# Every other pair of rows of the down blocks as seven products, and fewer low halves by adding DMA

## The chip, the cores and the metric

One NeuronCore of a Trainium2 chip runs the whole kernel. The metric is the time of one execution in device microseconds. Three runs of the kernel before took 2382.86, 2375.7 and 2385.11 us; the median, 2382.86, is the time before.

## What is computed

Two decoder layers on 256 tokens of width 2048 in float32. Each layer adds a mixer of attention heads and then an MLP to the residual x; a final RMSNorm ends it. The change touches the MLP alone:

```python
def squared_relu_mlp(h, w1, w2):
    return jnp.square(jax.nn.relu(h @ w1)) @ w2
...
    h = rmsnorm(x, ln_mlp[layer])
    x = x + squared_relu_mlp(h, mlp_w1[layer], mlp_w2[layer])
```

Here w1 is 2048 x 8192 and w2 is 8192 x 2048, 64 MB each in each layer.

## The kernel before

Every float32 operand is held as two fp32r halves: the high half is a cast, the low half is the operand less the high half. A product of two operands is three matmuls, high x high, high x low and low x high (`mm`, lines 180 to 186). `split` (149) makes both halves: ScalarE casts (150), VectorE subtracts (151). So most casts and subtracts, and most matmuls of the down products, carry these helper lines.

The MLP (`mlp`, 710) cuts the 8192 hidden columns into 16 units of 512, and the units into six chunks of 2, 3, 3, 3, 3 and 2 (`CHUNKS`, 713). A unit takes 8 up steps (`Up`, 780), one for each 256 rows of w1; each loads 512 KB, and its products go to four PSUM banks of the pool `acc` (811, 812). At the last of them `Unit.leave` (746) empties the banks: ScalarE copies and VectorE adds four times (750, 751), then ScalarE takes ReLU and square (752, 753). `Unit.build` (756) later makes the halves that the down products use as stationary operand, in parts that are done one a step.

The down product of a chunk goes by four blocks of 512 output columns, and in a block by pairs: a pair is 256 rows of w2, two to a unit, and one step. Two kinds of step exist. `Plain` (818) multiplies 2 row tiles x 2 token tiles x 512 columns: 12 matmuls of 512 columns. `Seven` (850) takes the same pair as a 2 x 2 by 2 x 2 product with seven products in place of eight: 21 matmuls of 256 columns, for which sums of weights (`sums`, 863, three VectorE adds into a tile T), sums of activations (the `s` tiles of `build`, 762 to 770) and a recombination at the block's end (`end`, 884: one ScalarE copy, six VectorE operations, two later adds into x) are needed. In the kernel before, the first three blocks of a chunk are all `Seven`, in four banks of the pools `psc` and `ptr`, and the fourth is all `Plain`, in the two banks of `psc`, from which VectorE adds into x (902). The last chunk is all `Plain` and stays as it is.

Raw weights come through six raw tiles of 512 KB (`raw_tile`, 143), loaded on SyncE's queue. High and low halves of 1024 columns take three tiles each (`half_tiles`, 146; tags wh and wl); steps of seven products take two wide tiles each (`wide_tiles`, 723; sh and sl). For the up steps of chunks 1 to 5 (`moved`), the low half is not made by VectorE: `early` (787) casts on ScalarE (791), writes the negated high half on ScalarE (792), and a DMA on GpSimd's queue adds the raw weights to it (793). The raw tile is free again when that DMA has landed.

The order of the work is written out by hand. `woven` (948) puts the up steps of chunk c + 1 between the down steps of chunk c, about one to one; that is a layer's woven stretch, 112 up and 112 down steps. The loop at 1001 then does, for the step at position p: load the step at p + 7, split the step at p + 2, the early halves of the step at p + 4, the sums of the step at p + 3, the products of p and what ends there, and one part of the waiting builds and adds (`later`). Each engine takes its instructions in that order.

Of the kernel before, what the change touches and what calls it, by code (L numbers as in the profile page):

```python
# [66 lines left out]
def decoder_trunk(ctx, tc, const, x_in, ln_mix, ln_mlp, ln_final, e_w_in, e_g_q, e_g_kv, e_w_uq, e_w_ukv, e_w_out,  # L67
# [10 lines left out]
    def nm(s):  # L78
        uid[0] += 1
        return f"{s}_{uid[0]}"  # L80
# [68 lines left out]
    def split(hi, lo, raw):  # L149
        nc.scalar.copy(hi, raw)  # L150
        nc.vector.tensor_tensor(lo, raw, hi.bitcast(F32), op=ALU.subtract)  # L151
# [558 lines left out]
    def mlp(layer, ss, done, tail=None):  # L710
# [3 lines left out]
        with ExitStack() as st:  # L714
# [21 lines left out]
            class Unit:  # L736
# [19 lines left out]
                def build(self):  # L756

                    def first():
                        self.halves = [pool.tile([P, 2, 8, 128], F32R, name=nm(h), tag=f"{h}{self.n}", bufs=1) for h in ("ah", "al")]
                        split(*(h[:, :, :4] for h in self.halves), self.a)  # L760

                    def second():
                        a = self.a
                        t = self.t = pool.tile([P, 2, 4, 128], F32, name=nm("s"), tag="s", bufs=1)
                        nc.vector.tensor_tensor(t[:, :, 0:2], a[:, :, 0:1].to_broadcast([P, 2, 2, 128]), a[:, :, 1:3], op=ALU.subtract)

                    def third():
                        a, t = self.a, self.t
                        nc.vector.tensor_tensor(t[:, :, 2], a[:, :, 1], t[:, :, 1], op=ALU.subtract)
                        nc.vector.tensor_tensor(t[:, :, 3], a[:, :, 3], t[:, :, 2], op=ALU.subtract)  # L770

                    def last():
                        split(*(h[:, :, 4:] for h in self.halves), self.t)

                    return [first] if self.c == len(CHUNKS) - 1 else [first, second, third, last]

                def slot(self, p, s):
                    return [h[:, p, s, :] for h in self.halves]

            class Up(Step):  # L780
# [6 lines left out]
                def early(self):  # L787

                    if self.moved:
                        hi, lo = self.w = half_tiles()  # L790
                        nc.scalar.copy(hi, self.raw)  # L791
                        nc.scalar.activation(lo, hi.bitcast(F32), AF.Copy, scale=-1.0)  # L792
                        nc.gpsimd.dma_start(lo, self.raw, accum_op=ALU.add)  # L793
# [56 lines left out]
            class Seven(Step):  # L850
# [5 lines left out]
                PRODUCTS = ((0, 0, 1, 1), (0, 1, 6, 6), (1, 0, 4, 5), (1, 1, 5, 4), (2, 0, 2, 7), (2, 1, 7, 2), (3, 0, 3, 3))  # L856

                def __init__(self, block, i, units, cs, c):
                    self.block, self.i, self.units, self.cs = block, i, units, cs
                    self.pairs = 2 * len(units)  # L860
                    self.src = rows(w2[:, cs], 4 * sum(CHUNKS[:c]) + 2 * i)

                def sums(self):
                    self.t = pool.tile([P, 1024], F32, name=nm("T"), tag="T", bufs=2)
# [10 lines left out]
                def product(self):  # L875
# [3 lines left out]
                    wh, wl = (w.rearrange("p (s n) -> p s n", n=256) for w in self.w)  # L879
                    for q, j, sa, sb in self.PRODUCTS:  # L880
                        mm(b["o"][q][:, j, :], self.units[i // 2].slot(i % 2, sa), (wh[:, sb - 1], wl[:, sb - 1]), i == 0 and j == 0,
                           i == self.pairs - 1, skip_group_check=True)

                def end(self):
# [3 lines left out]
                    (p1, p6), (p7, p5), (p4, p3), (p2, _) = ((b[:, 0, :], b[:, 1, :]) for b in o)  # L888
                    v = pool.tile([P, 2, 512], F32, name=nm("v"), tag="v", bufs=1)
                    c1, u2, u3, u4 = v[:, 0, 256:], v[:, 1, 256:], v[:, 0, :256], v[:, 1, :256]  # L890
                    nc.scalar.copy(c1, p1)
                    nc.vector.tensor_tensor(u2, p6, c1, op=ALU.subtract)
                    nc.vector.tensor_add(v[:, :, :256], o[1], u2.unsqueeze(1).to_broadcast([P, 2, 256]))
                    nc.vector.tensor_add(u2, p2, c1)
                    nc.vector.tensor_tensor(c1, p4, u3, op=ALU.subtract)
                    nc.vector.tensor_add(u3, p5, u3)
                    nc.vector.tensor_add(u4, p3, u4)
# [36 lines left out]
            def ups(c, moved):  # L934
                return [Up(u, i, moved) for u in units[c] for i in range(KT // 2)]

            def downs(c):
# [3 lines left out]
                for n in range(4):  # L941
                    block = {"of": psc}
                    cs = slice(n * 512, n * 512 + 512)
                    for i in range(2 * CHUNKS[c]):
                        seq.append(Seven(block, i, units[c], cs, c) if n < 3 else Plain(block, i, units[c], cs, c, True))
                return seq

            def woven(a, b):

                out, i = [], 0  # L950
                for j, s in enumerate(b):
                    while i < len(a) and i * len(b) <= j * len(a):
                        out.append(a[i])
                        i += 1
                    out.append(s)
                return out + a[i:]
# [143 lines left out]
```

## Time and profile before

| what | value |
|---|---|
| median of three runs | 2382.86 us |
| profiled execution: time, span of its instructions | 2385.53 us, 2383.8 us |
| mean granted TensorE clock, share of full speed | 0.977 |
| TensorE matmul busy | 2247.1 us |
| VectorE, ScalarE busy | 1574.4 us, 1443.8 us |
| read from HBM | 403.08 MB |
| mean rate of all DMA queues | 220 GB/s |

Busy time of an engine is the time in which one of its instructions runs; issuing and waiting do not count. Matmuls overlap, so a step is better measured from its first matmul to the first matmul of the next step. The granted clock is that of TensorE, as a share of 2.4 GHz. In the views, PE is TensorE, DVE is VectorE, ACT is ScalarE, POOL is GpSimd and SP is SyncE, a q after the name is its queue, and an arrow in a wait points to what ended it.

### The profile page before, as it was taken

Reading aid. Unit: us, or ns where it says so; the run is one execution under the profiler, and the core shown is the slowest. Engines: PE = TensorE matmul, PEld = TensorE weight load, DVE = VectorE, ACT = ScalarE, POOL = GpSimd, SP = SyncE. Lnnn points to the kernel's source line nnn. Section 1 sums busy time; section 2 is a strip of 40 time slices with the busy share of each in tenths; the row PEclk is TensorE's granted clock in tenths of the full one; section 3 lists DMA queues with packets and bytes.
Section 4 is the critical chain, followed back from the end, with each engine's and each line's share of the span. In section 5 each row is a group of like instructions: output and inputs, shape, how many; then the busy total and the mean of one; then the engine's idle time right before and its main releaser. Section 6 shows DMA issues by size and latency. Waiting matters only on the chain.

```text
span 2383.8 us, 35175 instructions
## 1 busy us (share of the span) xinstructions
PE 2247.1 (94%) x13590; PEld 1993.2 (84%) x13590; DVE 1574.4 (66%) x2505; ACT 1443.8 (61%) x1845; POOL 193.1 (8%) x228
## 2 busy tenths in 40 slices
PE   8999999898999999999999999998899999999898
PEld 7899988687888878788799999886788888887886
DVE  6777665555867767586675666555558577675866
ACT  6445444666867767676544444445677677776664
POOL 0000000011111111111000000001111111111110
PEclk9999999999999999999999999999999999999999
DMA  7554445699999999989565565456999999999884
GB/s 243 169 169 149 151 167 175 163 261 262 276 265 258 259 254 280 260 233 249 174 192 169 162 183 165 173 181 171 265 262 281 266 248 267 259 262 264 234 234 150
DMA packets 245860, 524.92 MB, mean 220 GB/s; under 512 B 18423, under 2 KB 23485, under 8 KB 245693
## 3 DMA queue, kind: packets, MB, share of 16 engines
q1 hardware_dynamic: 213436, 405.23, 51.3%
q0 software_dynamic: 32256, 117.45, 26.4%
q8 instruction: 106, 1.74, 0.3%
q14 instruction: 62, 0.50, 0.1%
HBM read 403.08 MB, written 2.10 MB: 170 GB/s over the span
## 4 chain that ended last, share of the span: by engine, by line
PE 52%; DMA 21%; DVE 12%; ACT 8%; issue 6%; SPq 0%; POOL 0%; DVEq 0%; ACTq 0%; POOLq 0%
PE bank L185 13%; PE bank L184 13%; PE bank L186 13%; DMA wl<-raw 11%; DMA raw<-in_mlp_w_dram 9%; PE bank L811 6%; DVE sl L151 4%; PE bank L812 3%; ACT wh L791 2%; ACT sh L150 2%; ACT wl L792 2%; DVE a L751 1%; DVE x L902 1%; ACT a L752 1%; DVE T L866 1%
## 5 line engine op out<-in xcount | busy, mean ns | idle before, releaser
L811 PE MATMUL bank<-xx,wh 128*128 128x512 f32 x2048 | 748.5, 403 | 5.0 <-DVE a L751 5.0
L812 PE MATMUL bank<-xx,wl 128*128 128x256 f32 x2048 | 587.2, 287 | 52.4 <-DMA wl<-raw 52.3
L151 DVE TENSOR_TENSOR wl<-raw,wh 128x1024 fp32r<-128x1024 f32 (+2 forms) x302 | 363.1, 1204 | 261.1 <-ACT wh L150 255.4
L150 ACT CAST wh<-raw 128x1024 fp32r<-128x1024 f32 (+2 forms) x302 | 311.2, 1033 | 351.9 <-PE bank L186 155.6
L184 PE MATMUL bank<-sh,ah 128*128 128x256 f32 (+1 forms) x1472 | 460.1, 313 | 35.4 <-DVE x L902 19.3
L185 PE MATMUL bank<-sl,ah 128*128 128x256 f32 (+1 forms) x1472 | 460.3, 313 | 15.5 <-DVE sl L151 15.3
L811 PEld LDWEIGHTS bank<-xx,wh 128*128 128x128 f32 x2048 | 393.6, 192 | 92.2 <-DVE a L751 7.2
L186 PE MATMUL bank<-sh,al 128*128 128x256 f32 (+1 forms) x1472 | 458.0, 311 | 8.1 <-DVE al L151 8.1
L812 PEld LDWEIGHTS bank<-xx,wl 128*128 128x128 f32 x2048 | 394.9, 193 | 69.6 <-DMA wl<-raw 67.0
L151 DVE TENSOR_TENSOR sl<-raw,sh 128x768 fp32r<-128x768 f32 (+1 forms) x241 | 248.7, 1032 | 241.6 <-ACT sh L150 240.8
L793 POOL DMA_DIRECT2D wl<-raw x224 | 192.9, 861 | 2120.3 <-ACT wl L792 1886.3
L791 ACT CAST wh<-raw 128x1024 fp32r<-128x1024 f32 x224 | 234.5, 1047 | 206.0 <-DMA raw<-in_mlp_w_dram 178.1
L184 PEld LDWEIGHTS bank<-sh,ah 128*128 128x128 f32 x1472 | 291.0, 198 | 60.6 <-ACT sh L150 13.6
L185 PEld LDWEIGHTS bank<-sl,ah 128*128 128x128 f32 x1472 | 291.3, 198 | 31.4 <-DVE sl L151 21.4
L186 PEld LDWEIGHTS bank<-sh,al 128*128 128x128 f32 x1472 | 291.9, 198 | 21.2 <-DVE al L151 9.1
L792 ACT ACTIVATE wl<-wh 128x1024 fp32r<-128x1024 f32 x224 | 237.6, 1061 | 7.1
L150 ACT CAST sh<-raw 128x768 fp32r<-128x768 f32 (+1 forms) x241 | 212.7, 883 | 44.6 <-PE bank L186 44.5
L150 ACT CAST sh<-T 128x1024 fp32r<-128x1024 f32 x168 | 176.2, 1049 | 67.3 <-DVE T L868 65.4
L185 PE MATMUL bank<-xx,wh 128*128 128x256 f32 x768 | 216.5, 282 | 0.0
L184 PE MATMUL bank<-xx,wh 128*128 128x256 f32 x768 | 216.3, 282 | 0.0
L186 PE MATMUL bank<-xx,wl 128*128 128x256 f32 x768 | 215.6, 282 | 0.0
L151 DVE TENSOR_TENSOR sl<-T,sh 128x1024 fp32r<-128x1024 f32 x168 | 205.6, 1224 | 11.7 <-ACT sh L150 7.2
(188 smaller groups left out, 3054.6 us busy)
## 6 DMA issues: line engine op xcount, KB each, us to landing
raw<-in_mlp_w_dram SPq DMA_DIRECT2D x510, 512.0 KB, 6.2
wl<-raw POOLq DMA_DIRECT2D x224, 512.0 KB, 7.1
raw<-in_o_w_in_dram SPq DMA_DIRECT2D x96, 512.0 KB, 3.8
raw<-in_e_w_in_dram SPq DMA_DIRECT2D x71, 512.0 KB, 3.5
raw<-in_e_w_out_dram SPq DMA_DIRECT2D x32, 512.0 KB, 3.5
raw<-in_o_w_out_dram SPq DMA_DIRECT2D x32, 512.0 KB, 3.5
raw<-in_e_w_uq_dram SPq DMA_DIRECT2D x8, 384.0 KB, 3.1
raw<-in_e_w_in_dram SPq DMA_DIRECT2D x8, 320.0 KB, 5.3
```

Source lines behind the costliest of these rows:

```text
L150: nc.scalar.copy(hi, raw)
L151: nc.vector.tensor_tensor(lo, raw, hi.bitcast(F32), op=ALU.subtract)
L184: nc.tensor.matmul(o, ah, bh, start=first, stop=False, **kw)
L185: nc.tensor.matmul(o, ah, bl, start=False, stop=False, **kw)
L186: nc.tensor.matmul(o, al, bh, start=False, stop=last, **kw)
L751: nc.vector.tensor_add(av[:, f], o[f][:, 0, :], av[:, f])
L752: nc.scalar.activation(self.a, self.a, AF.Relu)
L791: nc.scalar.copy(hi, self.raw)
L792: nc.scalar.activation(lo, hi.bitcast(F32), AF.Copy, scale=-1.0)
L793: nc.gpsimd.dma_start(lo, self.raw, accum_op=ALU.add)
L811: nc.tensor.matmul(u.o[f], wh[:, kk, fs], xx[:, k], start=k == 0, stop=False, skip_group_check=True)
L812: nc.tensor.matmul(u.o[f][:, 0, :], wl[:, kk, fs], xx[:, k, 0], start=False, stop=k == KT - 1, skip_group_check=True)
```

## The change

In all four blocks of chunks 0 to 4, even pairs are `Seven` and odd pairs are a new `Eight`: plain products that add to the last two of the same four banks, so that the seven products are laid out over the banks in another order and `end` recombines for all four blocks. Only the first pair of a unit needs sums of activations, so `build` has one part less and smaller ones. Of the eight up steps of a unit, numbers 1, 4 and 7 keep the adding DMA, with two tiles of their own for each half (mh, ml); the other five are split by ScalarE and VectorE two steps ahead. There is one T tile in place of two. `woven` now goes block by block: two up steps, then the block's pairs with the other up steps between them. A layer has 56 `Seven` and 56 `Eight` steps in its woven stretch, where it had 84 `Seven` and 28 `Plain`.

```diff
     def half_tiles(n=1024):
         return [wpool.tile([P, 1024], F32R, name=nm(h), tag=h, bufs=3)[:, :n] for h in ("wh", "wl")]
-    def split(hi, lo, raw):
+    def split(hi, lo, raw, on=nc.vector):
         nc.scalar.copy(hi, raw)
-        nc.vector.tensor_tensor(lo, raw, hi.bitcast(F32), op=ALU.subtract)
+        on.tensor_tensor(lo, raw, hi.bitcast(F32), op=ALU.subtract)
     class Weights:
...
                 def build(self):
                     def first():
-                        self.halves = [pool.tile([P, 2, 8, 128], F32R, name=nm(h), tag=f"{h}{self.n}", bufs=1) for h in ("ah", "al")]
-                        split(*(h[:, :, :4] for h in self.halves), self.a)
+                        self.halves = [pool.tile([P, 12, 128], F32R, name=nm(h), tag=f"{h}{self.n}", bufs=1) for h in ("ah", "al")]
+                        split(*(h[:, :8].rearrange("p (j s) n -> p j s n", j=2) for h in self.halves), self.a)
                     def second():
-                        a = self.a
-                        t = self.t = pool.tile([P, 2, 4, 128], F32, name=nm("s"), tag="s", bufs=1)
-                        nc.vector.tensor_tensor(t[:, :, 0:2], a[:, :, 0:1].to_broadcast([P, 2, 2, 128]), a[:, :, 1:3], op=ALU.subtract)
-                    def third():
-                        a, t = self.a, self.t
-                        nc.vector.tensor_tensor(t[:, :, 2], a[:, :, 1], t[:, :, 1], op=ALU.subtract)
-                        nc.vector.tensor_tensor(t[:, :, 3], a[:, :, 3], t[:, :, 2], op=ALU.subtract)
+                        a = self.a[:, 0]
+                        t = self.t = pool.tile([P, 4, 128], F32, name=nm("s"), tag="s", bufs=1)
+                        nc.vector.tensor_tensor(t[:, 0:2], a[:, 0:1].to_broadcast([P, 2, 128]), a[:, 1:3], op=ALU.subtract)
                     def last():
-                        split(*(h[:, :, 4:] for h in self.halves), self.t)
-                    return [first] if self.c == len(CHUNKS) - 1 else [first, second, third, last]
+                        a, t = self.a[:, 0], self.t
+                        nc.vector.tensor_tensor(t[:, 2], a[:, 1], t[:, 1], op=ALU.subtract)
+                        nc.vector.tensor_tensor(t[:, 3], a[:, 3], t[:, 2], op=ALU.subtract)
+                        split(*(h[:, 8:] for h in self.halves), self.t)
+                    return [first] if self.c == len(CHUNKS) - 1 else [first, second, last]
                 def slot(self, p, s):
-                    return [h[:, p, s, :] for h in self.halves]
+                    return [h[:, s + (4 * p if s < 4 else 4), :] for h in self.halves]
             class Up(Step):
...
                 def early(self):
                     if self.moved:
-                        hi, lo = self.w = half_tiles()
+                        hi, lo = self.w = [pool.tile([P, 1024], F32R, name=nm(h), tag=h, bufs=2) for h in ("mh", "ml")]
                         nc.scalar.copy(hi, self.raw)
                         nc.scalar.activation(lo, hi.bitcast(F32), AF.Copy, scale=-1.0)
                         nc.gpsimd.dma_start(lo, self.raw, accum_op=ALU.add)
...
-                PRODUCTS = ((0, 0, 1, 1), (0, 1, 6, 6), (1, 0, 4, 5), (1, 1, 5, 4), (2, 0, 2, 7), (2, 1, 7, 2), (3, 0, 3, 3))
+                PRODUCTS = ((0, 0, 1, 1), (0, 1, 6, 6), (1, 0, 4, 5), (1, 1, 5, 4), (2, 1, 2, 7), (3, 0, 7, 2), (3, 1, 3, 3))
                 def __init__(self, block, i, units, cs, c):
                     self.block, self.i, self.units, self.cs = block, i, units, cs
-                    self.pairs = 2 * len(units)
                     self.src = rows(w2[:, cs], 4 * sum(CHUNKS[:c]) + 2 * i)
                 def sums(self):
-                    self.t = pool.tile([P, 1024], F32, name=nm("T"), tag="T", bufs=2)
+                    self.t = pool.tile([P, 1024], F32, name=nm("T"), tag="T", bufs=1)
                     b, t = (v.rearrange("p (s n) -> p s n", n=256) for v in (self.raw, self.t))
                     nc.vector.tensor_add(t[:, 0:2], b[:, 1:3], b[:, 0:1].to_broadcast([P, 2, 256]))
                     nc.vector.tensor_add(t[:, 2], t[:, 0], b[:, 2])
...
                     if i == 0:
                         b["o"] = [bank((P, 2, 256), of) for of in (psc, psc, ptr, ptr)]
                     wh, wl = (w.rearrange("p (s n) -> p s n", n=256) for w in self.w)
+                    q0 = None
                     for q, j, sa, sb in self.PRODUCTS:
-                        mm(b["o"][q][:, j, :], self.units[i // 2].slot(i % 2, sa), (wh[:, sb - 1], wl[:, sb - 1]), i == 0 and j == 0,
-                           i == self.pairs - 1, skip_group_check=True)
+                        mm(b["o"][q][:, j, :], self.units[i // 2].slot(0, sa), (wh[:, sb - 1], wl[:, sb - 1]), i == 0 and q != q0,
+                           False, skip_group_check=True)
+                        q0 = q
+            class Eight(Plain):
+                def product(self):
+                    b, i = self.block, self.i
+                    wh, wl = (w.rearrange("p (k n) -> p k n", k=2) for w in self.w)
+                    for kk in range(2):
+                        for t in range(NT):
+                            mm(b["o"][2 + t].rearrange("p j n -> p (j n)"), self.units[i // 2].slot(i % 2, 2 * kk + t), (wh[:, kk], wl[:, kk]),
+                               False, False, skip_group_check=True)
                 def end(self):
                     if self.i < self.pairs - 1:
                         return
                     o = self.block["o"]
-                    (p1, p6), (p7, p5), (p4, p3), (p2, _) = ((b[:, 0, :], b[:, 1, :]) for b in o)
-                    v = pool.tile([P, 2, 512], F32, name=nm("v"), tag="v", bufs=1)
-                    c1, u2, u3, u4 = v[:, 0, 256:], v[:, 1, 256:], v[:, 0, :256], v[:, 1, :256]
-                    nc.scalar.copy(c1, p1)
-                    nc.vector.tensor_tensor(u2, p6, c1, op=ALU.subtract)
-                    nc.vector.tensor_add(v[:, :, :256], o[1], u2.unsqueeze(1).to_broadcast([P, 2, 256]))
-                    nc.vector.tensor_add(u2, p2, c1)
-                    nc.vector.tensor_tensor(c1, p4, u3, op=ALU.subtract)
-                    nc.vector.tensor_add(u3, p5, u3)
-                    nc.vector.tensor_add(u4, p3, u4)
+                    v = pool.tile([P, NT, 512], F32, name=nm("v"), tag="v", bufs=1)
+                    u = pool.tile([P, 1, 256], F32, name=nm("u"), tag="u", bufs=1)
+                    halves = v.rearrange("p t (j n) -> p (t j) n", j=2)
+                    nc.scalar.copy(halves[:, 3], o[0][:, 0, :])
+                    nc.vector.tensor_tensor(u[:, 0], o[0][:, 1, :], halves[:, 3], op=ALU.subtract)
+                    nc.vector.tensor_add(halves[:, 1:3], o[1], u.to_broadcast([P, 2, 256]))
+                    nc.vector.tensor_add(halves[:, 0], o[1][:, 1, :], halves[:, 1])
+                    nc.vector.tensor_add(halves[:, 0], o[2][:, 0, :], halves[:, 0])
+                    nc.vector.tensor_tensor(halves[:, 1], o[2][:, 1, :], halves[:, 1], op=ALU.subtract)
+                    nc.vector.tensor_add(halves[:, 2:4], o[3], halves[:, 2:4])
                     for t in range(NT):
                         later.append((None, partial(add, t, self.cs, v[:, t, :])))
...
             last = len(CHUNKS) - 1
             def ups(c, moved):
-                return [Up(u, i, moved) for u in units[c] for i in range(KT // 2)]
+                return [Up(u, i, moved and i % 3 == 1) for u in units[c] for i in range(KT // 2)]
             def downs(c):
                 seq = []
                 for n in range(4):
-                    block = {"of": psc}
+                    block = {}
                     cs = slice(n * 512, n * 512 + 512)
-                    for i in range(2 * CHUNKS[c]):
-                        seq.append(Seven(block, i, units[c], cs, c) if n < 3 else Plain(block, i, units[c], cs, c, True))
+                    seq.append([Eight(block, i, units[c], cs, c, False) if i % 2 else Seven(block, i, units[c], cs, c)
+                                for i in range(2 * CHUNKS[c])])
                 return seq
-            def woven(a, b):
-                out, i = [], 0
-                for j, s in enumerate(b):
-                    while i < len(a) and i * len(b) <= j * len(a):
-                        out.append(a[i])
-                        i += 1
-                    out.append(s)
-                return out + a[i:]
+            def woven(a, blocks):
+                out, n = [], len(blocks)
+                for j, b in enumerate(blocks):
+                    part = a[len(a) * j // n : len(a) * (j + 1) // n]
+                    rest, i = part[2:], 0
+                    out += part[:2]
+                    for k, s in enumerate(b):
+                        out.append(s)
+                        while i < len(rest) and i * len(b) < (k + 1) * len(rest):
+                            out.append(rest[i])
+                            i += 1
+                return out
             order = ups(0, False)
```

## Rows read from the trace of the kernel before

**Rows 1.** The page, parts 1 and 3: busy us (share) xinstructions; queue: packets, MB, share.
```profile
PE 2247.1 (94%) x13590; PEld 1993.2 (84%) x13590; DVE 1574.4 (66%) x2505; ACT 1443.8 (61%) x1845; POOL 193.1 (8%) x228
...
q1 hardware_dynamic: 213436, 405.23, 51.3%
q0 software_dynamic: 32256, 117.45, 26.4%
```

**Rows 2.** Windows, the two woven stretches: us, busy by engine, granted clock, DMA share, GB/s.
```profile
448.80:1141.50 692.70, 634.72 (x3885) 565.88 (x3884) 474.95 (x715) 479.51 (x546) 94.62 (x110) 0.96 0.94 254
1632.60:2326.00 693.40, 637.13 (x3887) 567.58 (x3886) 474.85 (x715) 479.12 (x546) 94.65 (x110) 0.96 0.95 255
```

**Rows 3.** Timeline of TensorE, first products of five steps: start us, us, engine, line, op.
```profile
703.44 0.39 PE L184 MATMUL bank<-sh,ah 128*128 128x512 f32 x1
...
706.21 0.40 PE L811 MATMUL bank<-xx,wh 128*128 128x512 f32 x1
...
752.30 0.28 PE L184 MATMUL bank<-sh,ah 128*128 128x256 f32 x1
...
754.81 0.39 PE L811 MATMUL bank<-xx,wh 128*128 128x512 f32 x1
...
757.62 0.28 PE L184 MATMUL bank<-sh,ah 128*128 128x256 f32 x1
```

**Rows 4.** Waits of TensorE, whole span: line <- releaser: us, times, longest us.
```profile
PE bank L812 <- DMA wl<-raw: 52.3, 38, 4.3
...
PE bank L184 <- DVE x L902: 19.3, 6, 4.0
...
PE bank L185 <- DVE sl L151: 15.3, 27, 0.8
...
PE bank L186 <- DVE al L151: 8.1, 4, 3.6
...
PE bank L184 <- ACT ah L150: 6.8, 4, 2.0
...
PE bank L184 <- DVE v L892: 5.1, 2, 2.6
...
PE bank L811 <- DVE a L751: 5.0, 5, 1.7
```

**Rows 5.** Timelines of ScalarE and TensorE, the end of a unit and what follows.
```profile
631.40 1.17 ACT L750 COPY a<-bank 128x256 f32<-128x256 f32 x4
...
635.00 1.06 ACT L753 ACTIVATE a<-a 128x1024 f32<-128x1024 f32 x1
...
636.84 0.38 PE L184 MATMUL bank<-sh,ah 128*128 128x256 f32 x1
...
639.64 0.42 PE L185 MATMUL bank<-sl,ah 128*128 128x256 f32 x1
...
642.63 0.44 PE L811 MATMUL bank<-xx,wh 128*128 128x512 f32 x1
```

**Rows 6.** Waits of SyncE's queue, whole span.
```profile
SPq L729 <- DMA wl<-raw: 874.9, 204, 9.7
```

**Rows 7.** Line 793, the 224 adding DMAs: issue to landing.
```profile
DMA to landing us min/median/max: 4.5/7.1/11.2
```

**Rows 8.** Timelines of ScalarE and VectorE, the end of a block of seven-product steps.
```profile
621.92 0.36 ACT L891 COPY v<-bank 128x256 f32<-128x256 f32 x1
...
623.18 0.42 DVE L892 TENSOR_TENSOR v<-bank,v 128x256 f32<-128x256 f32 x1
...
625.77 0.42 DVE L897 TENSOR_TENSOR v<-bank,v 128x256 f32<-128x256 f32 x1
626.10 0.74 DVE L902 SCALAR_TENSOR_TENSOR x<-v,rr,x 128x512 f32<-128x512 f32 x1
```

**Rows 9.** Lines by form, 480 to 1110 us: xcount | busy us, mean ns | idle.
```profile
L151 DVE TENSOR_TENSOR sl<-T,sh 128x1024 fp32r<-128x1024 f32 x80 | 97.9, 1224 | 5.4 <-ACT sh L150 3.4
...
L151 DVE TENSOR_TENSOR sl<-raw,sh 128x768 fp32r<-128x768 f32 x80 | 76.4, 955 | 63.1 <-ACT sh L150 62.9
```

## Prediction

> **What bounds the kernel now.** I read the page's busy shares first: TensorE is busy for 94% of the span, VectorE for 66%, ScalarE for 61%, and the GpSimd queue's transfers, the adding DMAs, take 26.4% of sixteen engines' span beside 51.3% for the loads [rows 1]. So TensorE is nearest to the bound, but a busy matmul says little, since matmuls overlap. The change touches only the two woven stretches, where up steps and down steps alternate. The view by windows gives their lengths: 692.7 and 693.4 us, together 1386.1, with a DMA share of 0.94 and 0.95 [rows 2].
>
> What these stretches would take without a wait comes from the timeline of TensorE, where a step's price is the distance from its first matmul to that of the next step. A step of seven products takes 754.81 - 752.30 = 2.51 us, an up step 757.62 - 754.81 = 2.81, a plain step 706.21 - 703.44 = 2.77 [rows 3]. The two layers weave 224 up steps with 168 seven-product steps and 56 plain ones: 224 x 2.81 + 168 x 2.51 + 56 x 2.77 = 629 + 422 + 155 = 1206 us. So 180 us are lost in 1386.
>
> The view of waits says to what. TensorE's idle time by releaser is 52.3 us for the low half that an adding DMA writes, 24.4 for VectorE's adds out of the down banks (19.3 + 5.1), 20.3 for VectorE's low halves and the adds that empty a unit's banks (15.3 + 5.0), and 14.9 for the first units' halves (8.1 + 6.8) [rows 4]. These 112 us are less than 180. The rest follows the waits: behind one, 128x256 matmuls take 0.42 us instead of 0.28, the lower of the two levels of the clock (1.2 instead of 2.4 GHz), and the granted clock of the stretches is 0.96 [rows 2, 5]. I spread it in proportion, a factor of 1.61: 84 us for the DMA, 39 for the down banks, 33 for unit ends, 24 for the start.
>
> **Why the DMA is late.** 405.23 MB of loads took 0.513 x 2383.8 = 1223 us of all sixteen engines, so 0.524 MB take 1.58 us; 224 adding DMAs took 0.264 x 2383.8 = 629 us, 2.81 each [rows 1]. Eight up and eight down steps ask for 16 x 1.58 + 8 x 2.81 = 47.8 us of transfer, while TensorE needs 8 x 2.81 + 6 x 2.51 + 2 x 2.77 = 43.1. The transfers want more time than TensorE gives them. The load queue shows the loop: SyncE waited 874.9 us, 204 times, for an adding DMA to give back a raw tile [rows 6], and such a DMA lands 7.1 us after its issue in the middle, 4.5 at best [rows 7].
>
> **The change, term by term** (both layers, against the profiled execution's own 2385.5 us, which is 2.7 above the median of the three runs).
>
> *Products.* 56 seven-product steps become plain: 56 x (2.77 - 2.51) = **+15 us**, all on TensorE's path. Here the trace disagrees with the Trainium skill, "TensorE: Matmul & The Clock Gate", section "Back-to-back issue gap": it gives columns / 2.4 + 2.5 ns for one matmul behind another, by which, as an estimate, a seven-product step is 21 x 109 ns = 2.29 us, a plain one 12 x 216 = 2.59, and the term +17, the sum 2 us higher. The rows decide.
>
> *Adding DMAs.* Of 224 there remain 84. Eight up and eight down steps then ask for 16 x 1.58 + 3 x 2.81 = 33.7 us of transfer against 8 x 2.81 + 4 x 2.51 + 4 x 2.77 = 43.6 on TensorE, 77%. Loads no longer stand behind raw tiles that an adding DMA holds: the other 140 are released by VectorE two steps ahead of their use. What stays late is the add whose ScalarE half is queued behind a unit's end. In the third block of each six-pair chunk the unit ends at the sixth step, and the moved up step five steps later gets its two ScalarE passes only after that: some 1.0 us, 3 chunks x 2 layers, 6 x 1.0 x 1.61 = 10 us. So 84 - 10: **-74 us**. The POOL queue holds nothing else that could wait behind.
>
> *Block ends.* All 40 blocks now end with one ScalarE copy and six VectorE operations (30 do today), and the next block's seven-product split stands behind them on VectorE. From first to last those six take 625.77 + 0.42 - 623.18 = 3.0 us [rows 8], an add into x 0.74 [rows 8]. The split behind needs 0.96 + 1.22 [rows 9]. If all of it began at the last product's end, it would last 0.4 + 3.0 + 0.7 + 2.2 = 6.3 us, against two up steps (5.6 us) and the one product (3 of 21 matmuls, 0.36) that needs only the first subtract: 0.3 late. But the last pair of a block is plain and writes only the third and fourth bank, and in the code an operation reads one bank's tile: ScalarE's copy (0.36 [rows 8]) and the first VectorE operations read banks that the pair before has finished and can run during the last pair. What is left behind the end is at most four of the six, about 1.9, and 0.7 + 2.2: 4.8 us, hidden under 5.6. Cost nothing; without that cover 0.3 to 2 us each.
>
> At the end of a chunk it is not free: the third unit's end stands ahead of the block's copy on ScalarE. In the trace a unit's end holds ScalarE from 631.40 to 636.0, 4.6 us; its own passes are 1.17 + 2 x 1.06 = 3.3, and more where VectorE's adds between them come late [rows 5]. I take 4.1, with 3.6 and 4.6 as ends. One plain step (2.77) runs beside it, so the chain of 6.3 us starts some 1.4 to 1.8 us after the last product, and the first seven-product step waits about 2.0. Three such chunk ends a layer: 6 x 2.0 x 1.61 = 19 us in place of 39, **-20 us**.
>
> *Unit ends.* Up weights are now cast and subtracted two steps ahead, so their splits stand behind a unit's end. A split of 1024 columns behind it is ready 4.1 + 1.0 + 1.2 = 6.3 us after the unit's last product; two steps and one matmul, 5.5 us, stand before its use. So 0.8 late where the unit ends as second step of a block (a plain split) and 0.8 where it ends as sixth (an up split), there with another 1.0 for the seven-product split that follows. I take 2.4 a layer for the first chunk's three units and 1.2 for the last woven chunk's two: 3 x (0.8 + 0.8 + 1.0) + 3.6 = 11.4 a layer, 22.8 x 1.61 = 37 us in place of 33, **+4 us**. With 4.6 it would be +20, with 3.6 about -12. These are the estimates I trust least, and the range carries them.
>
> *Builds, sums, start.* Building a unit loses a step, and its sums and split shrink to half; half of a 128x256 sum lies between 0 and its 0.42 [rows 8]. All of it is on VectorE and ScalarE between other work: nothing. Sums into one T tile rather than two: two seven-product steps never follow each other any more, so the tile is free: nothing. At the start TensorE gets one more up step to run (2.8 us) but the first seven-product split (2.2 us) now stands behind the norm and the builds: 0 between -4 and +4 for both layers.
>
> *VectorE as a whole.* It is busy 475 of 692.7 us [rows 2]. Per layer: 70 more up subtracts at 1.22 (+86), 28 seven-product steps less, each at least 0.96 + 3 x 0.42 (-62), 5 more block ends of 3.0 + 1.5 (+22), smaller builds (some -20): 501 of about 652, 77%. ScalarE loses 70 second passes. Neither becomes the bound on average.
>
> Sum: 15 - 74 - 20 + 4 = -75 us. 2385.5 - 75 = 2310.5, less 2.7 for the median: **2308 us**.
>
> **Rivals.**
> 1. *New waits hardly show* (faster still). Splits run far enough ahead that unit and chunk ends hide. For it: VectorE and ScalarE are idle three tenths of the stretches [rows 2]. Against: a unit's end costs 642.63 - 636.84 - 2.51 = 3.28 us in the step behind it today [rows 5]. Without the 10 + 19 + 37 us: 2308 - 66 = 2242.
> 2. *The remaining adds stay late.* They still hold raw tiles, and each passes ScalarE twice, the GpSimd queue, and 4.5 us or more of transfer. If half of today's 84 us stays: 2308 + 42 - 10 = 2340.
> 3. *VectorE's order makes every block end late* (slower). The mechanism: the six operations, the add and the split run in one queue, after the last plain pair instead of partly under it, with up subtracts (new on this queue) ahead of them. Its price is that of a split that arrives late today, 3.28 us with its slow clock: 40 x 3.28 - 19 = 112, so 2420. It decides from 75 / 40 = 1.9 us more per block end. For it: VectorE goes from 69% to 77%. Against: the early banks, and two up steps of cover.
> 4. *About even.* Rival 2 and two fifths of rival 3 together: 2308 + 32 + 45 = 2385.
> To the case that the change doesn't do what it says I give nothing: each of its parts issues fewer or more instructions that can be counted.
>
> **Numbers.** The forecast (2280 to 2330) gets 0.50, rival 1 0.15, rival 2 0.15, rival 4 0.10, rival 3 0.10. A measurement of this kernel tells about 0.5%, 12 us, from no change. So faster 0.80, same 0.10, slower 0.10. The range runs from the slow half of rival 1 (2245) to 2385, rival 4; it leaves out rival 3, half of rival 1 and half of rival 4, some 0.2.
>
> **What would show it.** Right: TensorE's wait for the adding DMA falls from 52 us to about 6; the DMA share of the stretches from 0.94 to about 0.8; the two stretches together last about 1310 us; 84 adding DMAs; no wait of the down products for VectorE's adds outside the chunk ends; VectorE 77% busy there. Wrong: down products that wait for the low halves of seven-product steps at every block start (rival 3), or a wait for adding DMAs above 20 us (rival 2).

## The result, and the profile after

The change takes 2283.3 us (median of four runs, 2282.0 to 2284.7) against 2381.9 for the kernel before beside it: a ratio of 0.9589, 95% interval 0.9568 to 0.961, 99 us faster. The forecast was 2308, 74 us faster; the time lies inside the range.

The page after, parts 1 and 3, answers to [rows 1]:

```profile
PE 2216.2 (97%) x13086; PEld 1947.4 (85%) x13086; DVE 1601.7 (70%) x2481; ACT 1245.5 (55%) x1659; POOL 72.6 (3%) x88
...
q1 hardware_dynamic: 213436, 405.23, 55.8%
q0 software_dynamic: 12096, 44.05, 10.7%
```

The windows view of the two woven stretches, columns as in [rows 2]:

```profile
445.70:1090.00 644.30, 622.15 (x3642) 545.11 (x3640) 485.99 (x701) 384.41 (x457) 35.25 (x41) 0.99 0.75 217
1578.80:2223.70 644.90, 622.51 (x3642) 545.22 (x3640) 486.12 (x701) 384.98 (x457) 35.29 (x41) 0.99 0.75 216
```

Together 1289 us. The windows of [rows 2] begin 3 us behind the stretch's first product; from that product, as here, the stretches before last 695.7 and 696.4 us, 1392. So the stretches are 103 us shorter and the profiled executions 102: all of the gain lies in them. TensorE alone needs 224 x 2.81 + 112 x 2.51 + 112 x 2.77 = 1221 us there; 68 us are lost, where 186 of 1392 were. VectorE is busy 75%, the DMA share is 0.75, the granted clock 0.99.

The waits of TensorE after, whole span, answer to [rows 4]:

```profile
PE bank L810 <- DMA ml<-raw: 16.9, 13, 2.3
PE bank L184 <- ACT sh L150: 13.6, 2, 6.8
PE bank L185 <- DVE sl L151: 8.0, 16, 1.0
PE bank L809 <- DVE a L751: 6.6, 2, 3.3
```

The wait for the adding DMA is down from 52.3 us to 16.9, and its longest from 4.3 to 2.3. No block's first down product waits for a bank any more (24.4 us before). The start still waits about as long (13.6 us, for the first seven-product split; before it was 14.9 us, for the units' halves). The last line is longer than before: in both layers an up step waits 3.3 us for a bank of the unit before it, where the longest such wait was 1.7 [rows 4]. The timelines of VectorE and TensorE show how:

```profile
563.63 0.42 DVE L904 TENSOR_TENSOR u<-bank,v 128x256 f32<-128x256 f32 x1
...
566.08 0.68 DVE L909 TENSOR_TENSOR v<-bank,v 128x512 f32<-128x512 f32 x1
566.67 0.74 DVE L914 SCALAR_TENSOR_TENSOR x<-v,rr,x 128x512 f32<-128x512 f32 x1
...
568.86 1.41 DVE L751 TENSOR_TENSOR a<-bank,a 128x256 f32<-128x256 f32 x4
```

```profile
569.33 0.79 PE L809 MATMUL bank<-xx,wh 128*128 128x512 f32 x1 [3.32 <-DVE a L751]
569.92 0.41 PE L810 MATMUL bank<-xx,wl 128*128 128x256 f32 x1
```

At the end of the first woven chunk a unit's end comes one step after a block's end. The six operations, the add into x and three sums stand ahead of the adds (751) that empty the unit's banks, and behind the wait TensorE runs at the lower level of its clock (0.41 us where 0.28 is usual). The windows view has a granted clock of 0.50 there:

```profile
569.30:572.50 3.20, 3.17 (x10) 2.69 (x11) 1.63 (x4) 2.17 (x3) 0.00 (x0) 0.50 0.52 191
```

### The profile page after: what moved, and what is told of

Read it like the earlier page. It is cut to its first block, busy times and chain, and to the rows that moved or that the text cites. A ratio compares the mean times of both kernels' runs of the same rounds, so it can differ in the third digit from the quotient of the medians.

```text
span 2282.2 us, 33668 instructions
## 1 busy us (share of the span) xinstructions
PE 2216.2 (97%) x13086; PEld 1947.4 (85%) x13086; DVE 1601.7 (70%) x2481; ACT 1245.5 (55%) x1659; POOL 72.6 (3%) x88
## 4 chain that ended last, share of the span: by engine, by line
PE 75%; DVE 10%; issue 6%; DMA 6%; ACT 3%; SPq 0%; DVEq 0%; POOLq 0%
PE bank L185 17%; PE bank L186 16%; PE bank L184 16%; PE bank L809 14%; PE bank L810 7%; DMA ml<-raw 3%; DVE wl L151 3%; DMA raw<-in_mlp_w_dram 2%; DVE sl L151 2%; PE pt L223 1%; ACT wh L150 1%; PE ps L445 1%; DVE x L914 1%; DVE al L151 1%; ACT ah L150 1%
## 5 line engine op out<-in xcount | busy, mean ns | idle before, releaser
L151 DVE TENSOR_TENSOR wl<-raw,wh 128x1024 fp32r<-128x1024 f32 (+3 forms) x554 | 665.7, 1211 | 389.1 <-ACT wh L150 381.1
L150 ACT CAST wh<-raw 128x1024 fp32r<-128x1024 f32 (+3 forms) x554 | 568.6, 1037 | 387.8 <-PE bank L186 162.8
L809 PE MATMUL bank<-xx,wh 128*128 128x512 f32 x1376 | 493.1, 398 | 6.6 <-DVE a L751 6.6
L184 PE MATMUL bank<-sh,ah 128*128 128x256 f32 (+1 forms) x856 | 250.2, 292 | 13.6 <-ACT sh L150 13.6
L185 PE MATMUL bank<-sl,ah 128*128 128x256 f32 (+1 forms) x856 | 251.7, 294 | 8.4 <-DVE sl L151 8.0
L186 PE MATMUL bank<-sh,al 128*128 128x256 f32 (+1 forms) x856 | 249.4, 291 | 0.0
L809 PE MATMUL bank<-xx,mh 128*128 128x512 f32 x672 | 243.4, 398 | 0.0
L810 PE MATMUL bank<-xx,ml 128*128 128x256 f32 x672 | 192.4, 286 | 17.0 <-DMA ml<-raw 16.9
L185 PE MATMUL bank<-wl,ah 128*128 128x512 f32 (+1 forms) x520 | 204.6, 393 | 1.4 <-DVE wl L151 1.4
L184 PE MATMUL bank<-wh,ah 128*128 128x512 f32 (+1 forms) x520 | 204.4, 393 | 0.0
L186 PE MATMUL bank<-wh,al 128*128 128x512 f32 (+1 forms) x520 | 203.5, 391 | 0.0
```

The source lines that it names most:

```text
L151: on.tensor_tensor(lo, raw, hi.bitcast(F32), op=ALU.subtract)
L184: nc.tensor.matmul(o, ah, bh, start=first, stop=False, **kw)
L185: nc.tensor.matmul(o, ah, bl, start=False, stop=False, **kw)
L186: nc.tensor.matmul(o, al, bh, start=False, stop=last, **kw)
L809: nc.tensor.matmul(u.o[f], wh[:, kk, fs], xx[:, k], start=k == 0, stop=False, skip_group_check=True)
L810: nc.tensor.matmul(u.o[f][:, 0, :], wl[:, kk, fs], xx[:, k, 0], start=False, stop=k == KT - 1, skip_group_check=True)
```

## The experiments

Three theories were set against each other: *transfers* (the gain is the adding DMAs taken away), *order* (the new weave and the handing over of banks), and *queues* (VectorE and ScalarE work in the order of issue, and what the seven products put there makes halves late). The expectations call the third one VectorE's or the queue theory. VectorE's busy time is of the whole span; "TensorE's own" is what both woven stretches take without a wait, by the step prices of [rows 3]. Of each edit only the main lines are shown.

| run | sevens, of 224 | adding DMAs | TensorE's own | VectorE busy | time |
|---|---|---|---|---|---|
| before | 168 | 224 | 1206 | 1574 | 2382 |
| e1 | 168 | 84 | 1206 | 1723 | 2338.7 |
| e5 (e1 in the new order) | 168 | 84 | 1206 | 1725 | 2355.9 |
| e2 | 112 | 224 | 1221 | 1447 | 2378.4 |
| after | 112 | 84 | 1221 | 1602 | 2283.3 |
| e4 (after in the old order) | 112 | 84 | 1221 | 1604 | 2286.2 |
| e3, e7 | 112 | 0 | 1221 | 1695, 1693 | 2345.7, 2309.9 |
| e12 | 0 | 224 | 1250 | 1034 | 2310.3 |
| e8 | 0 | 84 | 1250 | 1192 | 2257.8 |
| e10 | 0 | 0 | 1250 | 1290 | 2261.7 |
| e11 | 72 | 84 | 1231 | 1495 | 2239.6 |

**e1: only the adding DMAs go.**

```diff
-                return [Up(u, i, moved) for u in units[c] for i in range(KT // 2)]
+                return [Up(u, i, moved and i % 3 == 1) for u in units[c] for i in range(KT // 2)]
```

> The kernel before with one thing changed: only 3 of 8 up steps keep the adding DMA, in the old order and with the old products. Transfers theory (the gain is the adding DMAs taken away): TensorE's wait for them falls from 52 us to under 15, and the time falls by 45 to 80 us, to 2300 to 2335, though VectorE is now busy some 88% of the stretches. Order theory (the gain is in the new weave and the handing over of banks): 2360 or more. VectorE theory (old products and new subtracts together are too much for it): the DMA wait goes but waits for sl and wl take its place, 2350 to 2400.

2338.7 us, ratio 0.9817 (0.9797 to 0.9837): 47 us, just short of what transfers gave. TensorE's waits of this run:

```profile
PE bank L185 <- DVE sl L151: 21.0, 37, 1.1
PE bank L184 <- DVE x L902: 17.9, 6, 4.0
...
PE bank L184 <- DVE v L892: 8.1, 2, 4.1
PE bank L812 <- DMA wl<-raw: 7.3, 9, 1.2
...
PE bank L184 <- DVE v L896: 4.8, 6, 1.1
```

The wait for DMAs fell to 7.3 us, under the 15 that transfers had, but sl rose from 15.3 to 21.0 and the down banks, three lines together, from 26.5 (24.4 of [rows 4] and 2.1) to 30.8 us: VectorE is now busy 549 of 671 us of a stretch, 82%. Both theories hold a part.

**e2: the kernel after, with all adding DMAs back** (up steps in the three shared half tiles, plain pairs in the wide ones, as before).

```diff
-                return [Up(u, i, moved and i % 3 == 1) for u in units[c] for i in range(KT // 2)]
+                return [Up(u, i, moved) for u in units[c] for i in range(KT // 2)]
```

> The kernel after with all eight up steps by adding DMA again, in the tiles that the kernel before used (plain pairs in the wide tiles). Transfers theory: the DMA share goes back to 0.94, the wait for adding DMAs to 40 us or more, and the time rises by 50 to 80 us to 2335 to 2365. Order theory: under 2305.

2378.4 us, ratio 0.9972 (0.9957 to 0.9986): with products and order alone nearly nothing is won. TensorE's waits:

```profile
PE bank L810 <- DMA wl<-raw: 68.5, 55, 4.2
PE bank L185 <- DVE sl L151: 24.6, 33, 3.5
PE bank L184 <- ACT sh L150: 12.2, 8, 6.2
```

Order falls, and transfers expected too little: 95 us between this run and the kernel after, more than the 47 of e1. Each part of the change brings more with the other than alone. (The tiles differ too: the run has the shared tiles of before, so the 95 is not the DMA's alone. No run has the new products and 84 adding DMAs in the old tiles.)

**e4: the kernel after in the old order**, the old `woven` over the same down steps.

```diff
+                b = [s for block in blocks for s in block]
+                for j, s in enumerate(b):
+                    while i < len(a) and i * len(b) <= j * len(a):
```

> The kernel after with the order of before: one up step ahead of each down step in place of two at the head of a block. By the reading that the operations at a block's end are mostly early, one up step (2.8 us) covers the 1.9 us in which the last banks are emptied, and the split of the next block stands ahead of them: 2275 to 2300. Order theory: every block end waits, 40 x 1.5 us or more, 2340 or more.

2286.2 us, ratio 0.9597 (0.958 to 0.9614), not to be told from the kernel after. But the same time is made of other waits:

```profile
PE bank L184 <- DVE u L904: 16.1, 8, 2.8
...
PE bank L810 <- DMA ml<-raw: 3.2, 5, 1.0
```

Down products wait for banks again, 1.7 to 2.8 us at three chunk ends and at one block of the last chunk in each layer; at the other block ends one up step covers it, as expected. The wait for adding DMAs is 13.7 us shorter than in the kernel after. So the new order takes away the late banks and pays for it with late adding DMAs; on balance it brings nothing.

**e3 and e7: no adding DMA at all.** e3 makes every low half on VectorE. e7 does the same, but plain pairs get the two tiles for each half that the adding DMAs had.

```diff
             class Eight(Plain):
+                def split(self):
+                    self.w = [pool.tile([P, 1024], F32R, name=nm(h), tag=h, bufs=2) for h in ("mh", "ml")]
+                    split(*self.w, self.raw)
```

> The kernel after with no adding DMA at all: VectorE makes all low halves, 84 subtracts or 103 us more, 78 to 86% busy in the stretches. Transfers theory with slack on VectorE: the 17 us that TensorE still waits for adding DMAs go and little comes in their place, 2265 to 2285. VectorE theory: its queue comes late at unit ends and block ends, 2295 to 2340.

> The run without adding DMAs (2345.7 us) once more, with the two tiles for each half that the adding DMAs had given to the plain pairs, so that split weights have five tiles again and not three. If VectorE's 103 us more were what cost 62 us there: 2325 to 2350 again. If it was the lack of tiles (ScalarE's cast waits until TensorE has used a half, so the splits run less far ahead): the waits for sl and wl fall to under 20 us together and the time comes back to 2270 to 2295.

e3 took 2345.7 us (0.9844, 0.9826 to 0.9861), above even what the queues theory gave; e7 2309.9 (0.9696, 0.9681 to 0.9711), between its two cases. ScalarE's wait for a tile that TensorE still used, in e3 and then in e7:

```profile
ACT wh L150 <- PE bank L809: 148.8, 64, 4.2
```

```profile
ACT wh L150 <- PE bank L809: 53.1, 37, 4.0
```

and TensorE's for the low halves, in the same order:

```profile
PE bank L185 <- DVE sl L151: 41.9, 48, 3.1
```

```profile
PE bank L185 <- DVE sl L151: 31.5, 30, 3.1
```

So of the 62 us, 36 come back with the tiles. The other 27 stay with VectorE's 84 more subtracts, and the wait for sl is 31.5 us where the kernel after has 8.0. Three adding DMAs in eight are worth keeping here, partly for the tiles that come with them.

**e5: the kernel after with its products undone** (3 of 8 adding DMAs and the new order stay; the products, banks and tiles are those of before). The edit is shown against the kernel before.

```diff
-                return [Up(u, i, moved) for u in units[c] for i in range(KT // 2)]
+                return [Up(u, i, moved and i % 3 == 1) for u in units[c] for i in range(KT // 2)]
...
-                        seq.append(Seven(block, i, units[c], cs, c) if n < 3 else Plain(block, i, units[c], cs, c, True))
+                    seq.append([Seven(block, i, units[c], cs, c) if n < 3 else Plain(block, i, units[c], cs, c, True)
```

> The kernel after with its products undone: three blocks of seven-product steps and a plain one in its own banks, as before, but 3 of 8 adding DMAs (in the three shared half tiles) and the new order. TensorE has 14 us less to do than the kernel after. If the products themselves are what the kernel after pays or saves: 2269 by TensorE's time alone. If the seven-product steps cost more in the queues of VectorE and ScalarE than they save, as the all-plain runs say, it lies with the first run (2338.7, same products and adding DMAs in the old order): 2325 to 2350.

2355.9 us, ratio 0.989 (0.9867 to 0.9913): 73 us slower than the kernel after, though TensorE has 15 us less to do, and above the 2325 to 2350 expected. TensorE's waits name the queues:

```profile
PE bank L185 <- DVE sl L151: 42.3, 69, 1.1
PE bank L184 <- ACT sh L150: 24.0, 10, 8.9
PE bank L811 <- ACT wh L150: 12.2, 8, 2.9
```

Two things are mixed into the 73. With these products the new order costs 17 us (e1 has the old one). And the adding DMAs share the half tiles here. That lack hardly shows: ScalarE waits 67 us for a wh tile that TensorE still uses (39.3 and 28.0), 50.4 in the kernel after, 148.8 in e3. It was not tried apart. ScalarE's wait for a wide tile, though, is 77.9 us and 2.5 in the kernel after: three blocks in four have one seven-product step behind another, and each takes one of two such tiles.

**e8, e10 and e12: no seven products at all.** e8 is the kernel after with plain pairs only, in two banks; e10 the same without adding DMAs; e12 is the kernel before, its eight of eight adding DMAs and its order, with plain pairs only.

```diff
-                    seq.append([Eight(block, i, units[c], cs, c, False) if i % 2 else Seven(block, i, units[c], cs, c)
-                                for i in range(2 * CHUNKS[c])])
+                    seq.append([Plain(block, i, units[c], cs, c, i % 2 == 0) for i in range(2 * CHUNKS[c])])
```

> The kernel after with no seven-product steps at all: all pairs plain, in two banks. TensorE has 112 x 0.25 = 28 us more to do, VectorE some 250 us less. If TensorE's products are the bound of the kernel after, 2300 to 2315. If VectorE still sets most of what is lost in the kernel after, that loss goes and the sum is 2270 to 2295.

> The kernel before with all down pairs plain and nothing else: all eight up steps by adding DMA, old order. TensorE has 168 x 0.25 = 43 us more, VectorE is nearly idle. Transfers theory: eight up and eight down steps still ask for 47.8 us of transfer against 44.6 on TensorE, so the wait for adding DMAs stays above 40 us: 2370 to 2420. Queue theory (what TensorE lost in the kernel before was mostly set by the seven-product work in VectorE's and ScalarE's queues): the waits go, 2280 to 2330.

> The all-plain run (2257.8 us) without any adding DMA. With seven products that step cost 62 us, or 27 with five tiles. If VectorE has room once the seven products are gone, the 7.0 us of waits for adding DMAs go and nothing comes: 2248 to 2260. If the adding DMAs are needed whatever the products are: 2275 or more.

e8 took 2257.8 us (0.9476, 0.9462 to 0.949): 25 us faster than the kernel after, though TensorE has 29 us more to do, and faster than either case gave. Its stretches by windows, and all that TensorE waits for beyond 1.5 us outside the first loads:

```profile
445.70:1077.90 632.20, 626.56 (x3138) 526.51 (x3137) 284.38 (x308) 331.67 (x368) 35.25 (x41) 1.00 0.75 221
1566.00:2198.40 632.40, 626.77 (x3138) 526.48 (x3137) 284.36 (x308) 331.86 (x368) 35.30 (x41) 1.00 0.75 221
```

```profile
PE bank L810 <- DMA ml<-raw: 7.0, 6, 1.2
PE bank L185 <- DVE sl L151: 5.3, 6, 1.1
```

Together they are 1265 us against 1250 of TensorE's own: 15 lost, where the kernel after loses 68. Tiles, adding DMAs and order are those of the kernel after, so the difference is the seven products': their saving on TensorE is more than taken back by the waits that come with their work on VectorE and ScalarE. e10, 2261.7 us (0.9482, 0.9454 to 0.951), is just outside both of its cases and not to be told from e8: without seven products VectorE makes nearly all low halves in time (sl waits 8.9 us). e12, 2310.3 us (0.9686, 0.9653 to 0.972), is 75 us faster than the kernel before beside it (2385.0) with 44 us more on TensorE, and its wait for adding DMAs is

```profile
PE bank L812 <- DMA wl<-raw: 29.9, 27, 2.5
```

Queues expected that time. But 30 us of DMA waits stay, and e8, with 84 adding DMAs, their own tiles and the new order, is 52 us faster. That is near the 47 of e1, where only the adding DMAs went, and below the 95 between e2 and the kernel after.

**e6 and e9: what is left in the kernel after.** e6 makes ReLU and square one VectorE operation; e9 builds the second unit behind the first seven-product split.

```diff
-                    nc.scalar.activation(self.a, self.a, AF.Relu)
-                    nc.scalar.activation(self.a, self.a, AF.Square)
+                    nc.vector.scalar_tensor_tensor(self.a, self.a, 0.0, self.a, op0=ALU.max, op1=ALU.mult)
```

```diff
+                    if u.n:
+                        later.extend((u, part) for part in u.build())
```

> The kernel after with a unit's end shortened on ScalarE: its ReLU and square (two passes of 1.06 us) become one VectorE operation, maximum with 0 times itself (some 1.2 us), so that the splits behind a unit's end start about 0.9 us earlier. If what is left is set by ScalarE's queue behind a unit's end (28 units): the wait for adding DMAs (16.9 us) and for sl (8.0) fall, 2258 to 2276. If VectorE is what is short now, its 34 us more cancel this or cost: 2281 to 2295.

> The kernel after with the start of each MLP's woven stretch changed: the second unit is built behind the first seven-product split and not ahead of it, which frees VectorE some 2.3 us earlier for that split. TensorE waits 6.8 us there twice. Expected 2 x 2 to 2 x 4 us with the slow clock behind it: 2274 to 2280; if the wait is for something else, no change.

e6: 2267.6 us (0.9517, 0.9501 to 0.9533), as expected of ScalarE's queue behind a unit's end, though VectorE is 36 us busier. The waits for the adding DMA fall to 10.9 us, for sl to 1.4; the one at the start rises from 13.6 to 16.2. e9: 2279.0 us (0.9565, 0.955 to 0.9579); its interval overlaps that of the kernel after, but the wait that it aimed at went from 13.6 to 7.8 us, so its 4 us are likely, not certain.

**e11: a version that beats both.** Seven products only in blocks 1 to 3 of the chunks after the first, every other pair; all else plain; e6's operation.

```diff
+                    if c == 0 or n == 3:
+                        seq.append([Plain(block, i, units[c], cs, c, i % 2 == 0) for i in range(2 * CHUNKS[c])])
+                        continue
```

> A mixture meant to beat both: seven-product steps only where they are not next to a start or a chunk's end (blocks 1 to 3 of chunks 1 to 4, 72 steps in place of 112 in the kernel after), the rest plain, and ReLU and square in one VectorE operation. TensorE has 40 x 0.25 = 10 us more than the kernel after and 18 less than the all-plain run. If a seven-product step pays away from those places: 2238 to 2252. If its work in the queues costs what it saves everywhere: 2255 to 2270.

2239.6 us, ratio 0.9391 (0.9363 to 0.9418), in the first of its cases. What TensorE still waits for most, outside the first loads:

```profile
PE bank L185 <- DVE sl L151: 4.8, 2, 2.4
...
PE bank L808 <- DVE a L751: 3.7, 2, 1.9
```

It is 18 us under e8, about what TensorE's own time has (1250 - 1231), and 28 under e6, which has 40 more of them. The second difference shows that the steps left out cost more than they saved. The first is what one would see if a seven-product step pays where VectorE has nothing else to catch up with, but e11 also has e6's operation, and no run has all plain pairs with it. That operation could have taken some of the 15 us that e8 loses: the wait for adding DMAs is 1.1 us here and 7.0 in e8. So that these steps pay is likely, and by how much is not shown.

## Why the prediction was right, and where it was not

*What it got right.* The stretches, the count of what they lose, and that most of it goes: 90 us were expected to stay (10 behind adding DMAs, 19 at chunk ends, 37 at unit ends, 24 at the start); 68 stayed (by the distances between steps 20 behind unit ends and late adds, 24 at chunk ends, 20 at the starts, 4 elsewhere, most of it in the new plain steps: 2.79 us, not 2.77). The products' +15 is in TensorE's own time. Block ends at nothing is confirmed by the waits after: no down product waits for a bank. The 84 adding DMAs, the DMA share (0.75 for about 0.8), VectorE (75% for 77%) and the raw tiles came as said; SyncE's wait for adding DMAs fell from 874.9 us [rows 6] to

```profile
SPq L729 <- DMA ml<-raw: 271.2, 50, 11.8
SPq L827 <- DMA ml<-raw: 172.7, 34, 10.3
```

One sign did not come: TensorE's wait for the adding DMA was to fall to about 6 us and is 16.9.

*What the size missed.* Two terms of the sum. First, unit ends with the late adds were put at 37 + 10 us, from 28.8 us of waiting (22.8 + 6); the steps with such waits lose some 20 in the kernel after, from 14 us of waiting. The late adds are there, 7.8 us for 6. Of the rest 6 us are left: the up split of the sixth step is never late, the plain split 0.2 to 0.4 where 0.8 was said, the first chunk's units not at all. The timelines of ScalarE, GpSimd and TensorE at a unit's end in a third block:

```profile
651.65 0.37 ACT L750 COPY a<-bank 128x256 f32<-128x256 f32 x1 [4.63 <-PE bank L810]
...
655.73 1.06 ACT L753 ACTIVATE a<-a 128x1024 f32<-128x1024 f32 x1
...
658.70 1.06 ACT L790 ACTIVATE ml<-mh 128x1024 fp32r<-128x1024 f32 x1
```

```profile
660.06 0.86 POOL L791 DMA_DIRECT2D ml<-raw  x1 [21.56 <-ACT ml L790]
```

```profile
662.91 0.39 PE L185 MATMUL bank<-sl,ah 128*128 128x256 f32 x1 [0.55 <-DVE sl L151]
...
666.61 0.38 PE L810 MATMUL bank<-xx,ml 128*128 128x256 f32 x1 [1.16 <-DMA ml<-raw]
```

The seven-product split is 0.55 late and the moved up step 1.16, where 1.0 and 1.0 were said. The factor of 1.61 for the slow clock does not fit here either. TensorE stays at the full clock through both waits:

```profile
661.70:669.30 7.60, 5.89 (x39) 5.04 (x38) 6.01 (x7) 4.38 (x5) 0.00 (x0) 1.00 0.84 192
```

Still the two steps take 0.81 and 1.45 us longer, 0.25 to 0.3 more than the idle time shown, so 14 us of waiting make 20.

Second, chunk ends cost 24 us, not 19, and that the two lie so near is luck. The wait that the forecast named, of the first seven-product step for the chain of block-end operations, does not occur in the kernel after. At the six chunk ends for which it was counted, the second of the two up steps at the head waits for its adding DMA, 1.1 to 2.3 us (9.2 us in all, 14 lost). One of them:

```profile
709.44 0.39 PE L810 MATMUL bank<-xx,ml 128*128 128x256 f32 x1 [1.41 <-DMA ml<-raw]
```

At the first chunk's end, put at nothing but a late split, the unit's banks come late (10 lost in both layers). With one up step at the head (e4) the forecast wait is there, 1.7 to 2.8 us at the same six ends.

*Where the working failed though the sum held.* The step "Adding DMAs: -74 us" credits their removal alone. e1 shows that alone it brings 47, since the up subtracts then fall into VectorE's and ScalarE's queues, which the 168 seven-product steps fill. And the step "Products: +15", with "VectorE as a whole: neither becomes the bound on average", gave the halving of the seven products in these queues no gain. 52 us lie between e1 and e4, which have the same number of adding DMAs and the old order, and 73 between e5 and the kernel after; in both pairs the half tiles differ too. Without that difference, e8 and e12 show the same: leaving out all seven-product steps gains 25 and 75 us. An average share of 77% was the wrong test: VectorE at 82% (e1) already leaves TensorE waiting for halves, because the splits wait in one order behind sums, recombinations and unit ends. "Order" (-20 for handing over) is right in that the waits for down banks are gone, but waits for adding DMAs come in their place, and by itself the order brings 3 us at most (e4).

*The rivals.* Rival 2 is out by its own sign, but not by much: the wait for adding DMAs is 16.9 us, under its 20 and far above 6. Rival 3's mechanism is rare in the kernel after: apart from the start, a block's first step waits for its low halves at one block of the last chunk in each layer, 0.8 us. e5 comes near its effect: seven-product halves late 69 times, and 73 us slower. Rival 1 is partly true: the new waits hide better than the sum had it, and the time, 2283.3, lies 25 us below the forecast on the way to its 2242. About that time is what e11 reaches, by other steps.

*Open.* Whether VectorE's length or the hand-over between ScalarE and VectorE matters more in a seven-product step (its second cast waits on the sums, and all later casts behind it) was not tried separately. Nor were the tiles in e1, e2 and e5, or all plain pairs with e6's operation.

## What to carry to other kernels

A scheme that saves products on the busiest engine must be charged with all it puts into the in-order queues of the others, at the places where these have a burst to work off: here seven products for eight saved 0.26 us a step and cost more, and a kernel that kept them away from starts and chunk ends (with e6's operation) was the fastest. When two resources both limit a stretch (transfers and VectorE here), relieving one by loading the other shows only part of the gain; look for the pair of edits that does both, and test each alone. An engine's mean busy share is a poor bound for a queue in order: compare instead each half's due time with what stands ahead of it.

## What was not expected of the hardware

An adding DMA within on-chip memory took 0.107 x 2282.2 / 84 = 2.9 us of all sixteen engines for 512 KB, where a load of as much from HBM takes 0.558 x 2282.2 / 773 = 1.6, and taking away 140 of 224 hardly shortened its landing (7.0 us in the middle, 7.1 before [rows 7]):

```profile
DMA to landing us min/median/max: 4.8/7.0/11.2
```

The least is 4.8, where it was 4.5 [rows 7]. The loads of the MLP's weights did land earlier: 4.9 us in the middle on the page, 6.2 before.
